# A gated linear recurrence: pairs of tokens within 32 in two rounds of column-tiled matmuls, sample states on four column tiles

## The chip, the cores and the metric

The kernel runs on one core of a Trainium2 chip. A core has TensorE (PE in the profile; PEld is its weight load), VectorE (DVE), ScalarE (ACT), GpSimd (POOL) and SyncE (SP), which issues DMAs. TensorE reads SBUF and writes PSUM. The metric is the device time of one launch in microseconds (us); lower is better. Everything is f32, or f32r, the one-pass form of f32 on TensorE, in which the large matmuls run three times over a high and a low part.

## The reference, cut to what matters

Two layers. Layer 0 mixes tokens by causal pooling, layer 1 by HGRN2, a gated linear recurrence; each is followed by a gated ConvFFN. 512 prompt tokens and 8 samples of 4 new tokens (with a state each) go through together. The change lies in the recurrence of layer 1, with 8 heads of 128 x 128:

```python
def step(S, xs):                       # per chunk, per head
    qc, kc, vc, gc = xs                # gc = log of the decay f
    b = jnp.cumsum(gc, axis=2)
    o_inter = jnp.einsum('bhtd,bhde->bhte', qc * jnp.exp(b), S)
    diff = b[:, :, :, None, :] - b[:, :, None, :, :]
    decay = jnp.where(causal, jnp.exp(jnp.where(causal, diff, 0.0)), 0.0)
    a = jnp.einsum('bhtd,bhsd,bhtsd->bhts', qc, kc, decay)
    o = o_inter + jnp.einsum('bhts,bhse->bhte', a, vc)
    ...
    S = jnp.exp(b_last[:, :, 0, :])[..., None] * S + jnp.einsum('bhsd,bhse->bhde', kc * jnp.exp(b_last - b), vc)
```

`a[t, s]` holds, for each pair of tokens with s <= t, the sum over 128 channels of q[t] k[s] times the product of the decays f between them.

## The kernel before, in words

**Order of work.** Every operation is recorded first (`Plan.record`, the only line of the profile with nearly all instructions, L304) with a cost in microseconds (`Plan.cost`), and a list scheduler (`Plan.emit`) then writes the engines' orders: of what is ready by its own estimate, the operation with the longest tail goes next. Between the matmuls of a projection (`block`, 48 matmuls of 256 or 288 columns), a `tick` after every three adds `PACE` to a counter, and each time it reaches 1 one more step of the recurrence is recorded. An engine keeps its written order: if an instruction's input is late, those behind it wait.

**Layer 1.** The projections for f, q, i and g of each head run as such blocks; after a head's i, `attention(h)` queues its steps: load, transposes, diag, seven levels, ktrans, states, output, sstates, back. Head after head, they are interleaved with the blocks of later heads.

**Pairs by levels.** The matrix `A` (per 128-token chunk, 128 x 128, s on partitions, t on columns) is put together by distance. `diag` gives pairs s = t: K^T q over a whole chunk, of which only the diagonal is kept, by a product with the identity. Level w (1, 2, 4, ..., 64) gives the pairs in which s lies in the left and t in the right half of a block of 2w tokens. For this q and K are scaled step by step, at level w each right half of q by the decays of the left block of w, and each left half of K by those of the right one (`qv`, `kv`); the block decays are products of two each (`fn`). A full chunk of K (128 weight columns) meets 64 columns of q, and DVE copies the wanted blocks of the 128 x 64 result into A under a mask (`copy_predicated`). diag and w = 1 share a matmul of 192 columns for each of four chunks (the columns of q and of the scaled q side by side in the tile `q2`); so do w = 4 and w = 8. From w = 16 (`BLKW`) each block is a matmul of its own, 128 x w by w, and ScalarE copies it into A. The 32 samples' tokens have their own diag, w = 1 and w = 2 matmuls (tile `As`).

**States and output.** `states` makes the chunk states S; `output` sums A V (4 matmuls), the samples' As V, the samples' q against their 8 states, each with a masked copy of q that is zero but for its 4 of 32 columns (`qm`, 8 matmuls on PSUM partitions 0 to 31), and q S (3). `back` transposes the normed result, 4 chunks and the samples' 32 rows.

**Names in rows.** `ps`: PSUM of the projections; `pa`: PSUM tiles of the recurrence and of grouped blocks; `pr`: PSUM of the norms (`colsums` adds up squares with 32 columns of ones, on PSUM partitions 0, 32, 64 and 96 in turn); `t`: a ring of 24 tiles (q, K, F, V, states, ...); `cs`: constants (identity, ones, masks); `wl`, `wh`: low and high part of weights; `fst`/`q2`: one tile that serves the FFN and the recurrence in turn; `lbm`: lower bounds; `R`: the norm's factors.

Of the kernel before, what the change touches and what calls it, by code (L numbers as in the profile page):

```python
# [17 lines left out]
P = 128  # L18
D = 1024
KT = 8  # L20
SEQ = 512
# [16 lines left out]
LEVELS = (1, 2, 4, 8, 16, 32, 64)  # L38
# [10 lines left out]
PACE = 0.3  # L49
MERGE = 4  # L50
BLKW = 16
# [16 lines left out]
C_ID, C_ONE, C_SB, C_MASK, C_BM = 0, 128, 256, 256 + 192, 256 + 192 + 448  # L68
NCST = C_BM + NB

class Plan:
# [84 lines left out]
    def cost(eng, name, args, kw):  # L156
# [181 lines left out]
def trunk_step(ctx: ExitStack, tc: _tile.TileContext, xT, xp, xs, spool, s0, fctx, par, gb0, cst, bands,  # L338
# [8 lines left out]
    tp = ctx.enter_context(tc.tile_pool(name="tp", bufs=24))  # L347
# [498 lines left out]
    def ffn(li, XH, XL, res, enter, mtile, leave, n_ahead, hv=HV):  # L846

        R = res.rnext
        cst_t = rp.tile([P, 2 * NPAIR * 18], F32, tag="fst", name="fst", bufs=1)
# [160 lines left out]

    def lower_bounds():
# [29 lines left out]
    qm = one.tile([P, NB * 36], F32, name="qm")  # L1041
    DVE.memset(qm, 0.0)
    q2 = rp.tile([P, 2 * NPAIR * 18], F32, tag="fst", name="q2", bufs=1)[:, 0:768]
# [32 lines left out]
    def attention(h):  # L1076
# [30 lines left out]
        def diag():  # L1107

            qq = q2.rearrange("p (c t) -> p c t", c=4)
            ACT.activation(qq[:, :, 0:P], q[:, 0:SEQ].rearrange("p (c t) -> p c t", c=4), AF.Identity)  # L1110
            pd = [ps1(), ps1()]
            PE.matmul(pd[1][0:NS, 384:384 + NS], samp(K), samp(q), start=True, stop=True, skip_group_check=True)
            DVE.tensor_tensor(q, q, F, op=ALU.mult)
            ACT.activation(qq[:, :, P:192], q[:, 0:SEQ].rearrange("p (c t r) -> p c t r", c=4, r=2)[:, :, :, 1], AF.Identity)
            A = tt((P, 4, P))
            As = sm.tile([P, NS], F32, tag="As", name="As", bufs=2)
            st["A"], st["As"] = A, As
            mk = cs[:, C_MASK:C_MASK + 64].bitcast(I32)
# [3 lines left out]
            PE.matmul(pd[1][0:NS, 384 + NS:384 + NS + HS], samp(K), samp(q).rearrange("p (n r) -> p n r", r=2)[:, :, 1],  # L1122
                      start=True, stop=True, skip_group_check=True)
            for a in range(2):
                v = pd[a][:, 0:384].rearrange("p (c t) -> p c t", c=2)
                Aa = A[:, 2 * a:2 * a + 2, :]
                DVE.tensor_tensor(Aa, v[:, :, 0:P], ident.unsqueeze(1).broadcast_to([P, 2, P]), op=ALU.mult)
                DVE.copy_predicated(Aa.rearrange("p c (t r) -> p c t r", r=2)[:, :, :, 1], mk.unsqueeze(1).broadcast_to([P, 2, 64]), v[:, :, P:192])
            DVE.tensor_tensor(As[0:NS], pd[1][0:NS, 384:384 + NS], ident[0:NS, 0:NS], op=ALU.mult)
            DVE.copy_predicated(As[0:NS].rearrange("p (n r) -> p n r", r=2)[:, :, 1], mk[0:NS, 0:HS],  # L1130
                                pd[1][0:NS, 384 + NS:384 + NS + HS])
            st["F"] = F
            st["fl"], st["fo"] = tt(), 0

# [3 lines left out]
        def level(li):  # L1138
            w = LEVELS[li]
            nb = 64 // w  # L1140
            if li and w not in (MERGE, MERGE * 2):
                pl = ps1()
            smp = w < 4
            if w in (1, MERGE * 2):
                pass
            elif w == MERGE:

                wide = st["wide"] = [ps1(), ps1()]
                z = q2.rearrange("p (c t) -> p c t", c=4)
                qc = q[:, 0:SEQ].rearrange("p (c t) -> p c t", c=4)  # L1150

                def half(t, v):
                    return t.rearrange("p c (n r v) -> p c n r v", r=2, v=v)[:, :, :, 1, :]
                ACT.activation(z[:, :, 0:64].rearrange("p c (n v) -> p c n v", v=w), half(qc, w), AF.Identity)
                F0 = st["F"][:, 0:SEQ // w].rearrange("p (c n) -> p c n", c=4)
                DVE.tensor_tensor(half(qc, w), half(qc, w), F0[:, :, 0::2].unsqueeze(3).broadcast_to([P, 4, nb, w]),
                                  op=ALU.mult)
                zb, zc = (z[:, :, a:a + 64].rearrange("p c (n v) -> p c n v", v=2 * w) for a in (64, 128))
                ACT.activation(zb, half(qc, 2 * w), AF.Identity)
                DVE.tensor_tensor(zc, half(qc, 2 * w), F0[:, :, 1::4].unsqueeze(3).broadcast_to([P, 4, nb // 2, 2 * w]),  # L1160
                                  op=ALU.mult)
                for c in range(4):
                    PE.matmul(wide[c // 2][:, (c % 2) * 192:(c % 2 + 1) * 192], chunk(K, c), z[:, c, :], start=True,
                              stop=True, skip_group_check=True)
                for a in range(2):
                    src = wide[a][:, 0:384].rearrange("p (c t) -> p c t", c=2)
                    Aa = st["A"][:, 2 * a:2 * a + 2, :]
                    for col, v, slot in ((0, w, li), (64, 2 * w, li + 1), (128, 2 * w, 5)):
                        mk = cs[:, C_MASK + slot * 64:C_MASK + (slot + 1) * 64].bitcast(I32)
                        DVE.copy_predicated(half(Aa, v), mk.rearrange("p (n v) -> p n v", v=v).unsqueeze(1).broadcast_to(  # L1170
                            [P, 2, 64 // v, v]), src[:, :, col:col + 64].rearrange("p c (n v) -> p c n v", v=v))
            elif w >= BLKW:

                for j in range(0, P, 2 * w):
                    for c in range(4):
                        PE.matmul(pl[j:j + w, c * w:(c + 1) * w], chunk(K, c)[:, j:j + w],
                                  chunk(q, c)[:, j + w:j + 2 * w], start=True, stop=True)
                for j in range(0, P, 2 * w):
                    ACT.activation(st["A"][j:j + w, :, j + w:j + 2 * w],
                                   pl[j:j + w, 0:4 * w].rearrange("p (c t) -> p c t", c=4), AF.Identity)  # L1180
            else:
                for c in range(4):
                    PE.matmul(pl[:, c * 64:(c + 1) * 64].rearrange("p (n w) -> p n w", w=w), chunk(K, c),
                              oddv(chunk(q, c), w)[:, :, 1, :], start=True, stop=True)
                mk = cs[:, C_MASK + li * 64:C_MASK + (li + 1) * 64].bitcast(I32)
                if smp:
                    PE.matmul(pl[0:NS, 256:256 + HS].rearrange("p (n w) -> p n w", w=w), samp(K),
                              oddv(samp(q), w)[:, :, 1, :], start=True, stop=True)
                mk4 = mk.rearrange("p (n w) -> p n w", w=w).unsqueeze(1).broadcast_to([P, 4, nb, w])
                Av = st["A"].rearrange("p c (n r w) -> p c n r w", r=2, w=w)[:, :, :, 1, :]  # L1190
                DVE.copy_predicated(Av, mk4, pl[:, 0:256].rearrange("p (c n w) -> p c n w", c=4, w=w))
                if smp:
                    DVE.copy_predicated(oddv(st["As"][0:NS], w)[:, :, 1, :],
                                        mk[0:NS, 0:HS].rearrange("p (n w) -> p n w", w=w),
                                        pl[0:NS, 256:256 + HS].rearrange("p (n w) -> p n w", w=w))

            Fw = st["F"]
            if w <= 2:
                nbt = TOK // (2 * w)
                qv, kv = oddv(q, w)[:, :, 1, :], oddv(K, w)[:, :, 0, :]  # L1200
                fv = Fw.rearrange("p (n r) -> p n r", r=2)
                fe = fv[:, :, 0:1].broadcast_to([P, nbt, w])
                fo = fv[:, :, 1:2].broadcast_to([P, nbt, w])
                Fn = st["fl"][:, st["fo"]:st["fo"] + nbt]
                st["fo"] += nbt
# [301 lines left out]
```

## Time and profile before

| | |
|---|---|
| Median of 3 runs (lowest to highest) | 1246.05 us (1242.43 to 1247.79) |
| Profiled execution: time, span | 1243.85 us, 1242.1 us |
| Granted TensorE clock | 0.994 |
| Time from HBM and to it | 110.95 MB read, 8.31 MB written, 96 GB/s over the span |
| Recurrence (windows of the trace) | about 503 to 769 us |

"Busy" is a share of the span; matmuls are pipelined, so what a matmul costs is told by the distance between starts, not by its length. A row of the timeline has the start, the time, the engine, the line, the operation, out<-in by the tiles' names, the form (rows * weight columns, then out) and the count; after [ ] stands idle time before it. An f32 matmul shows as two instructions there and as one in the written order.

### The profile page before, as it was taken

How to read it: one execution, taken by the hardware profiler on the slowest of the kernel's cores; microseconds unless marked ns; L12 is line 12 of the kernel's file. 1: busy time of each engine (PE TensorE's matmuls, PEld its weight loads, DVE VectorE, ACT ScalarE, POOL GpSimd, SP SyncE). 2: the span in 40 equal slices, each digit the busy share in tenths (PEclk: the TensorE clock that was granted, in tenths of full speed). 3: DMA queues.
4: the chain of work that ended last, by engine and by line, in shares of the span. 5: the costliest groups of instructions: out<-in, count | busy, mean ns of one | idle time of the engine just before them, and what ended most of it. 6: DMA issues, size and time to landing. Idle time of an engine off the chain costs nothing.

```text
span 1242.1 us, 24777 instructions
## 1 busy us (share of the span) xinstructions
PE 1223.4 (98%) x9932; PEld 1187.3 (96%) x9932; DVE 795.1 (64%) x1834; ACT 545.3 (44%) x1083; POOL 212.2 (17%) x510
## 2 busy tenths in 40 slices
PE   8999999999999999999999999999999999999996
PEld 7899999999999988999999999999999999999995
DVE  6787725774577565677777887376762566457745
ACT  4754434442344554444444444465443344234441
POOL 3331101110011141011111211143110111011113
PEclk9999999999999999999999999999999999999998
DMA  9622222222222463322222123364222222322202
GB/s 324 155 88 85 86 85 86 96 78 90 96 84 92 153 142 71 102 80 79 80 96 80 63 71 100 102 137 101 87 85 97 88 85 75 100 86 89 84 29 72
DMA packets 43218, 120.49 MB, mean 97 GB/s; under 512 B 5338, under 2 KB 9818, under 8 KB 43096
## 3 DMA queue, kind: packets, MB, share of 16 engines
q1 hardware_dynamic: 30336, 91.87, 22.5%
q0 software_dynamic: 12624, 27.01, 9.1%
q8 instruction: 78, 1.28, 0.4%
q14 instruction: 36, 0.29, 0.1%
q10 hardware_dynamic: 144, 0.05, 0.0%
HBM read 110.95 MB, written 8.31 MB: 96 GB/s over the span
## 4 chain that ended last, share of the span: by engine, by line
PE 95%; DVE 2%; DMA 2%; ACT 1%; issue 0%; SPq 0%; DVEq 0%; ACTq 0%
PE ps L304 73%; PE pa L304 20%; PE pr L304 2%; DVE m L304 1%; DVE t L304 1%; DMA k<-xp 1%; DMA t<-pw 1%; DMA k<-wup 0%; ACT t L304 0%; SPq L304 0%; ACT wh L304 0%; DVE c L304 0%; ACT m L304 0%; DVE x L304 0%; DVEq L1488 0%
## 5 line engine op out<-in xcount | busy, mean ns | idle before, releaser
L304 ACT ACTIVATE wh<-raw 128x512 fp32r<-128x512 f32 (+1 forms) x312 | 193.1, 620 | 342.4 <-PE ps L304 330.9
L304 PE MATMUL ps<-xh,wh 128*128 128x256 f32 (+1 forms) x1072 | 312.4, 292 | 0.0
L304 PE MATMUL ps<-xh,wl 128*128 128x256 f32 (+1 forms) x1072 | 311.7, 291 | 0.0
L304 PE MATMUL ps<-xl,wh 128*128 128x256 f32 (+1 forms) x1072 | 311.5, 291 | 0.0
L304 DVE TENSOR_TENSOR wl<-raw,wh 128x512 fp32r<-128x512 f32 (+1 forms) x312 | 210.3, 675 | 133.1 <-ACT wh L304 129.2
L304 PE MATMUL ps<-t,wh 128*128 128x272 f32 x1184 | 223.4, 288 | 0.9 <-ACT m L304 0.7
L304 PEld LDWEIGHTS ps<-xh,wl 128*128 128x128 f32 x1072 | 202.2, 189 | 2.4 <-issue 1.4
L304 PEld LDWEIGHTS ps<-xh,wh 128*128 128x128 f32 x1072 | 201.6, 188 | 2.5 <-issue 1.3
L304 PEld LDWEIGHTS ps<-xl,wh 128*128 128x128 f32 x1072 | 202.2, 189 | 1.2 <-issue 0.5
L304 PE MATMUL ps<-oh,wl 128*128 128x256 f32 (+2 forms) x688 | 198.1, 288 | 0.0
L304 PE MATMUL ps<-k,wh 128*128 128x256 f32 (+2 forms) x688 | 197.7, 287 | 0.0
L304 PE MATMUL ps<-oh,wh 128*128 128x256 f32 (+2 forms) x688 | 197.3, 287 | 0.0
L304 DVE TENSOR_TENSOR t<-t 128x512 f32<-128x512 f32 (+7 forms) x332 | 146.4, 461 | 63.8 <-ACT t L304 45.0
L304 PEld LDWEIGHTS ps<-t,wh 128*128 128x128 f32 x1184 | 185.4, 188 | 1.8 <-ACT m L304 1.2
L304 DVE SCALAR_TENSOR_TENSOR t<-t,prm 128x560 f32<-128x560 f32 (+1 forms) x184 | 147.6, 805 | 35.7 <-ACT t L304 32.9
L304 PE MATMUL ps<-t,wl 128*128 128x272 f32 x592 | 170.3, 288 | 0.0
L304 POOL COPY fst<-t 128x2 f32<-128x2 f32 (+1 forms) x176 | 72.9, 443 | 442.9 <-DVE t L304 442.6
L304 DVE TENSOR_TENSOR t<-ps,R 128x512 f32<-128x512 f32 (+1 forms) x216 | 86.2, 434 | 77.1 <-PE ps L304 73.2
L304 PEld LDWEIGHTS ps<-k,wh 128*128 128x128 f32 x688 | 129.5, 188 | 0.5 <-issue 0.5
L304 PEld LDWEIGHTS ps<-oh,wl 128*128 128x128 f32 x688 | 129.7, 188 | 0.0
L304 PEld LDWEIGHTS ps<-oh,wh 128*128 128x128 f32 x688 | 129.6, 188 | 0.0
L304 ACT ACTIVATE t<-t 128x560 f32<-128x560 f32 (+4 forms) x137 | 83.1, 616 | 95.5 <-DVE t L304 94.5
(169 smaller groups left out, 1703.9 us busy)
## 6 DMA issues: line engine op xcount, KB each, us to landing
raw<-wup SPq DMA_DIRECT2D x78, 512.0 KB, 3.3
raw<-wdn SPq DMA_DIRECT2D x32, 448.0 KB, 3.3
raw<-win SPq DMA_DIRECT2D x26, 512.0 KB, 3.3
raw<-wdn SPq DMA_DIRECT2D x16, 512.0 KB, 3.2
wh<-wup POOLq DMA_DIRECT2D x16, 256.0 KB, 4.0
wl<-wup POOLq DMA_DIRECT2D x16, 256.0 KB, 5.1
t<-s POOLq DMA_DIRECT2D x16, 256.0 KB, 3.9
o_hs<-t POOLq DMA_DIRECT2D x16, 256.0 KB, 2.4
```

Source lines behind the costliest of these rows:

```text
L304: o[1](*o[3], **o[4])
```

## The change

Pairs within 32 tokens no longer use whole chunks. diag and the levels 1 to 8 become two rounds over the 16 blocks of 32 tokens: a matmul has one block's 32 columns of K as weights, and block g of a chunk writes PSUM partitions 32g to 32g + 31, so that four consecutive matmuls use the four column tiles of the array. Round A (diag, w = 1, w = 2; 80 columns) also takes the 32 samples' tokens as a 17th block; round B (w = 4, w = 8) has 48 columns. The pairs between the first and last quarter of a block of four (or 16) come from columns scaled once more (`zv(64, 2)`, `zv(32, 8)`). Results are collected in a tile `Al` of 4 x 32 columns under masks of 32 columns, then four ScalarE copies put them into the blocks on the diagonal of A. A is now one tile for all heads, zeroed once on GpSimd, as is qm, which holds two groups of four samples. The samples' q times state go four at a time to four column tiles, each with 32 columns (4 samples' tokens in the second half, others in the first); As is split likewise; the way back transposes 128 rows. Recording is paced at 0.25 instead of 0.3 with 12 steps in place of 15, the ring t has 22 tiles, and the planner's cost of narrow matmuls is another.

```diff
-LEVELS = (1, 2, 4, 8, 16, 32, 64)
+LOCAL = 32
+ROUND_A, ROUND_B = 80, 48
-PACE = 0.3
+PACE = 0.25
...
-                return n / 2400 + 0.01
+                return max(n / 2400 + 0.01, 0.0018 * m)
...
-    tp = ctx.enter_context(tc.tile_pool(name="tp", bufs=24))
+    tp = ctx.enter_context(tc.tile_pool(name="tp", bufs=22))
...
+                POOL.memset(A, 0.0)
+                POOL.memset(qm, 0.0)
...
-        def diag():
...
-            for c in range(4):
-                PE.matmul(pd[c // 2][:, (c % 2) * 192:(c % 2 + 1) * 192], chunk(K, c), qq[:, c, :], start=True,
-                          stop=True, skip_group_check=True)
...
+        def round_a():
+            z = q2[:, 0:17 * ROUND_A].rearrange("p (b t) -> p b t", t=ROUND_A)
...
+            ACT.activation(z[:, :, 0:LOCAL], q.rearrange("p (b t) -> p b t", t=LOCAL), AF.Identity)
+            DVE.tensor_tensor(q, q, F, op=ALU.mult)
+            ACT.activation(zv(32, 1), by_block(upper(q, 1)), AF.Identity)
+            scale(q, 1, 1, F)
+            hi = by_block(upper(q, 2))
+            ACT.activation(zv(48, 2), hi, AF.Identity)
+            DVE.tensor_tensor(zv(64, 2), hi, by_block(quarter(F, 1, 1)).broadcast_to([P, 17, 8, 2]), op=ALU.mult)
+            pl = ps1()
+            for c in range(4):
+                for g in range(4):
+                    b = 4 * c + g
+                    PE.matmul(pl[32 * g:32 * g + 32, c * ROUND_A:(c + 1) * ROUND_A], K[:, 32 * b:32 * b + 32], z[:, b, :],
+                              start=True, stop=True, skip_group_check=True)
+            PE.matmul(pl[0:NS, 4 * ROUND_A:5 * ROUND_A], samp(K), z[:, 16, :], start=True, stop=True, skip_group_check=True)
+            Al = sm.tile([P, 4, LOCAL], F32, tag="Al", name="Al", bufs=2)
...
+            scale(K, 1, 0, F)
+            products(1)
+            scale(q, 2, 1, st["F"])
+            scale(K, 2, 0, st["F"])
+            products(2)
...
+        def round_b():
...
+            for c in range(4):
+                for g in range(4):
+                    b = 4 * c + g
+                    PE.matmul(pl[32 * g:32 * g + 32, c * ROUND_B:(c + 1) * ROUND_B], K[:, 32 * b:32 * b + 32], z[:, b, :],
+                              start=True, stop=True, skip_group_check=True)
...
+            for j in range(0, P, LOCAL):
+                ACT.activation(A[j:j + LOCAL, :, j:j + LOCAL], st["Al"][j:j + LOCAL], AF.Identity)
...
         def output():
...
-            PE.matmul(po2[0:NS, 0:P], st["As"][0:NS], st["Vs"][0:NS], start=True, stop=False)
-            for b in range(NB):
-                PE.matmul(po2[0:NS, 0:P], st["qm"][:, b * NS:(b + 1) * NS], st["s0"][b // 4][:, b % 4, :],
-                          start=False, stop=(b == NB - 1))
...
+            for a in range(2):
+                for g in range(4):
+                    PE.matmul(po2[32 * g:32 * g + 32, 0:P], qm[:, a, g, :], st["s0"][a][:, g, :], start=(a == 0), stop=False,
+                              skip_group_check=True)
+            for g in range(4):
+                PE.matmul(po2[32 * g:32 * g + 8, 0:P], st["As"][0:NS, 8 * g:8 * g + 8], st["Vs"][0:NS], start=False, stop=True,
+                          skip_group_check=True)
...
-            PE.transpose(pq2[:, 0:NS], st["ons"][0:NS], ident[0:NS, 0:NS])
+            PE.transpose(pq2[:, 0:P], st["ons"], ident)
```

What TensorE's written order holds for the first head's pairs up to the level w = 16, before (`q_861` is the tile q2; the lines left out are projection matmuls):

```order
L304 MATMUL pa<-t 32x32
...
L304 MATMUL pa<-t 32x16
...
L304 MATMUL pa<-q_861,t 128x192 x4
...
L304 MATMUL pa<-t 128x64 x4
L304 MATMUL pa<-t 32x16
...
L304 MATMUL pa<-q_861,t 128x192 x4
...
L304 MATMUL pa<-t 16x16 x16
```

And the same piece of the changed order (`q_862` is q2); between the two rounds stand 16 projection matmuls:

```order
L304 MATMUL pa<-q_862,t 32x80 x17
...
L304 MATMUL pa<-q_862,t 32x48 x16
...
L304 MATMUL pa<-t 16x16 x16
```

Five bursts ahead of w = 16 have become two, and the samples' bursts of one matmul are gone.

The first head's output on TensorE, before:

```order
L304 MATMUL pa<-t 128x128 x8
L304 MATMUL pa<-t,As 32x128
L304 MATMUL pa<-t,qm 32x128 x8
L304 MATMUL pa<-t 128x128 x3
```

and after, where the state products (`states`) stand 12 projection matmuls ahead:

```order
L304 MATMUL pa<-t 128x128 x4
...
L304 MATMUL pa<-t,A 128x128 x4
L304 MATMUL pa<-t 128x128 x3
L304 MATMUL pa<-t,qm 32x128 x8
L304 MATMUL pa<-t,As 8x128 x4
```

The samples' products moved behind the full-width ones, and As is four narrow matmuls.

VectorE's changed order around the first head's rounds; the first four rows stand between round A and round B (K scaled, q scaled, K scaled, q2 written), the others after them:

```order
L304 TENSOR_TENSOR t<-t 128x272
L304 TENSOR_TENSOR t<-t 128x64x4
L304 TENSOR_TENSOR t<-t 128x136x2
L304 TENSOR_TENSOR q_862<-t 128x16x16
L304 TENSOR_TENSOR Al<-pa,cs 128x128
L304 TENSOR_TENSOR t<-t 128x32x8
L304 TENSOR_TENSOR As<-pa,cs 32x2x4x4
L304 COPY_PREDICATED Al<-cs,pa 128x64
L304 COPY_PREDICATED As<-cs,pa 32x2x4x2
L304 TENSOR_TENSOR t<-ps,R_226 128x512
```

What round B needs was put ahead of the masked copies of round A's results.

More of the change, by code (lines that the diff above doesn't have):

```diff
@@ L848, in ffn @@
         R = res.rnext
-        cst_t = rp.tile([P, 2 * NPAIR * 18], F32, tag="fst", name="fst", bufs=1)
+        cst_t = rp.tile([P, 17 * ROUND_A], F32, tag="fst", name="fst", bufs=1)[:, 0:2 * NPAIR * 18]
         if li == 0:
@@ L1009, in trunk_step @@
     lbm = one.tile([P, 8, KT], F32, name="lbm")
+    A = one.tile([P, 4, P], F32, name="A")
+    qm = one.tile([P, 2, 4, LOCAL], F32, name="qm")
     def lower_bounds():
@@ L1040, in trunk_step @@
     hd = {}
-    qm = one.tile([P, NB * 36], F32, name="qm")
-    DVE.memset(qm, 0.0)
-    q2 = rp.tile([P, 2 * NPAIR * 18], F32, tag="fst", name="q2", bufs=1)[:, 0:768]
+    q2 = rp.tile([P, 17 * ROUND_A], F32, tag="fst", name="q2", bufs=1)
     def proj(ps):
@@ L1105, in transposes @@
             st["V"], st["Vst"], st["Vs"] = V, VV[:, 0, :], VV[:, 1, :]
-        def diag():
[L1109 to L1118, printed above, removed]
-            for c in range(4):
-                PE.matmul(pd[c // 2][:, (c % 2) * 192:(c % 2 + 1) * 192], chunk(K, c), qq[:, c, :], start=True,
-                          stop=True, skip_group_check=True)
[L1122 to L1133, printed above, removed]
@@ L1135, in oddv @@
         def oddv(t, w):
             return t.rearrange("p (n r w) -> p n r w", r=2, w=w)
[L1138 to L1172, printed above, removed]
-                for j in range(0, P, 2 * w):
[L1175 to L1205, printed above, removed]
-                f0, f1, fn = fv[:, :, 0], fv[:, :, 1], Fn
-            else:
-                nbt = SEQ // (2 * w)
-                qv, kv = oddv(q[:, 0:SEQ], w)[:, :, 1, :], oddv(K[:, 0:SEQ], w)[:, :, 0, :]
-                fv = Fw[:, 0:2 * nbt].rearrange("p (n r) -> p n r", r=2)
-                fe = fv[:, :, 0:1].broadcast_to([P, nbt, w])
-                fo = fv[:, :, 1:2].broadcast_to([P, nbt, w])
-                Fn = st["fl"][:, st["fo"]:st["fo"] + nbt]
-                st["fo"] += nbt
-                f0, f1, fn = fv[:, :, 0], fv[:, :, 1], Fn
-            if w != MERGE:
-                DVE.tensor_tensor(qv, qv, fe, op=ALU.mult)
-            DVE.tensor_tensor(kv, kv, fo, op=ALU.mult)
-            DVE.tensor_tensor(fn, f0, f1, op=ALU.mult)
-            st["F"] = Fn
-            if w == 2:
-                st["F4"] = Fn
@@ new lines, in quarter, with upper, products, scale @@
+        def quarter(t, w, r):
+            return t.rearrange("p (n r w) -> p n r w", r=4, w=w)[:, :, r, :]
+        def upper(t, w):
+            return oddv(t, w)[:, :, 1, :]
+        def products(w):
+            f = st["F"].rearrange("p (n r) -> p n r", r=2)
+            n = f.shape[1]
+            fn = st["fl"][:, st["fo"]:st["fo"] + n]
+            st["fo"] += n
+            DVE.tensor_tensor(fn, f[:, :, 0], f[:, :, 1], op=ALU.mult)
+            st["F"] = fn
+        def scale(t, w, r, f):
+            tv = oddv(t, w)[:, :, r, :]
+            fv = f.rearrange("p (n r) -> p n r", r=2)[:, :, 1 - r:2 - r].broadcast_to(list(tv.shape))
+            DVE.tensor_tensor(tv, tv, fv, op=ALU.mult)
@@ new lines, in level @@
+        def level(w):
+            pl = ps1()
+            for c in range(4):
+                for j in range(0, P, 2 * w):
+                    PE.matmul(pl[j:j + w, c * w:(c + 1) * w], chunk(K, c)[:, j:j + w], chunk(q, c)[:, j + w:j + 2 * w],
+                              start=True, stop=True, skip_group_check=True)
+            for j in range(0, P, 2 * w):
+                ACT.activation(A[j:j + w, :, j + w:j + 2 * w], pl[j:j + w, 0:4 * w].rearrange("p (c t) -> p c t", c=4), AF.Identity)
+            scale(q[:, 0:SEQ], w, 1, st["F"])
+            scale(K[:, 0:SEQ], w, 0, st["F"])
+            products(w)
@@ L1264, in output @@
                           skip_group_check=True)
+            for a in range(2):
+                for g in range(4):
[4 more added lines that the diff above has]
+                          skip_group_check=True)
             on, ons = tt((P, 4, P)), tt((P, P))
             ss, r, w, z, a, b = (sm.tile([P, 5], F32, tag=f"o{q}", name="o", bufs=2) for q in range(6))
-            DVE.memset(ss[:, 4:5], 0.0)
             for c in range(4):
                 ACT.activation(on[:, c, :], po[:, c * P:(c + 1) * P], AF.Square, accum_out=ss[:, c:c + 1])
-            ACT.activation(ons[0:NS], po2[0:NS, 0:P], AF.Square, accum_out=ss[0:NS, 4:5])
+            ACT.activation(ons, po2[:, 0:P], AF.Square, accum_out=ss[:, 4:5])
             rstd_into(r, ss, 1.0 / P, w, z, a, b)
@@ L1295, in back @@
                 PE.transpose(pq[:, c * P:(c + 1) * P], st["on"][:, c, :], ident)
-            PE.transpose(pq2[:, 0:NS], st["ons"][0:NS], ident[0:NS, 0:NS])
+            PE.transpose(pq2[:, 0:P], st["ons"], ident)
             o = kslot(F32)
             ACT.activation(o[:, 0:SEQ], pq, AF.Identity)
-            ACT.activation(o[:, SEQ:TOK], pq2[:, 0:NS], AF.Identity)
+            ACT.activation(o[:, SEQ:TOK].rearrange("p (h g t) -> p g h t", h=2, g=4),
+                           pq2[:, 0:P].rearrange("p (g x) -> p g x", g=4)[:, :, 0:8].rearrange("p g (h t) -> p g h t", h=2), AF.Identity)
             hd[h]["on"] = o
-        return [load, transposes, diag] + [lambda li=li: level(li) for li in range(len(LEVELS))] + \
+        return [load, transposes, round_a, round_b] + [lambda w=w: level(w) for w in (16, 32, 64)] + \
             [ktrans, states, output, sstates, back]
```

79 lines of the change are left out of this document (64 added, 15 removed).

## The prediction

> **What bounds the kernel now.** I read the page first (busy shares, then the chain of waits), then the windows of the stage that the change touches, then TensorE's waits in it, and last its timeline.
>
> ```profile
> PE 1223.4 (98%) x9932; PEld 1187.3 (96%) x9932; DVE 795.1 (64%) x1834; ACT 545.3 (44%) x1083; POOL 212.2 (17%) x510
> PE 95%; DVE 2%; DMA 2%; ACT 1%; issue 0%; SPq 0%; DVEq 0%; ACTq 0%
> 503.00:769.00 266.00, 265.00 (x2360) 249.98 (x2359) 202.85 (x603) 115.67 (x344) 37.26 (x67) 1.00 0.24 81
> PE pa L304 <- DVE t L304: 1.0, 2, 0.7
> ```
>
> The second row is the chain of waits by engine: 95% of the span is TensorE following TensorE. The third is the stretch in which the eight heads' recurrences run (columns: length, then busy time and count of PE, PEld, DVE, ACT and POOL, granted clock, DMA share, GB/s): PE is busy 265.0 of 266.0 us at full clock. The fourth is all that PE waits there, 1.0 us in two waits. So a microsecond of TensorE work taken out of this stage is a microsecond off the end, as long as VectorE and ScalarE still deliver in time; and the whole question is what the matmuls of the recurrence cost TensorE before and after.
>
> **What they cost before.** The recurrence's matmuls stand as small bursts between the 256- and 288-column matmuls of the projection. This is the timeline of PE for the first head (start, time, form, instructions; an f32 matmul shows as two, called passes here).
>
> ```profile
> 504.85 0.28 PE L304 MATMUL ps<-xl,wh 128*128 128x256 f32 x1
> 504.97 0.28 PE L304 MATMUL ps<-xh,wl 128*128 128x256 f32 x1
> 505.18 0.25 PE L304 MATMUL pa<-t 128*32 128x32 f32 x2
> 505.35 0.40 PE L304 MATMUL ps<-xh,wh 128*128 128x288 f32 x1
> 505.59 0.29 PE L304 MATMUL ps<-xl,wh 128*128 128x288 f32 x1
> 505.72 0.29 PE L304 MATMUL ps<-xh,wl 128*128 128x288 f32 x1
> ...
> 507.30 0.23 PE L304 MATMUL pa<-t 128*32 128x16 f32 x2
> ...
> 508.06 1.46 PE L304 MATMUL pa<-q,t 128*128 128x192 f32 x8
> 509.22 0.43 PE L304 MATMUL ps<-xh,wh 128*128 128x288 f32 x1
> 509.49 0.29 PE L304 MATMUL ps<-xl,wh 128*128 128x288 f32 x1
> ...
> 510.61 1.17 PE L304 MATMUL pa<-t 128*128 128x64 f32 x10
> 511.71 0.39 PE L304 MATMUL ps<-xl,wh 128*128 128x256 f32 x1
> 511.93 0.28 PE L304 MATMUL ps<-xh,wl 128*128 128x256 f32 x1
> ...
> 515.20 1.46 PE L304 MATMUL pa<-q,t 128*128 128x192 f32 x8
> ```
>
> A projection matmul's own pace is 0.12 us at 256 columns (504.85 to 504.97) and 0.13 at 288 (505.59 to 505.72). A burst's price is what it adds to that pace. The samples' 32x32 matmul: from 504.97 to 505.59 pass 0.62 us, of which 0.12 + 0.13 are two projection matmuls, so it costs 0.37, although its arithmetic is tiny. The 16-column one (507.30) is the same burst with 0.23 us in place of 0.25: 0.35. The burst of four 192-column products: 509.49 - 508.06 - 0.13 = 1.30; the second one, same form and same 1.46, again 1.30. The w=2 level: 511.93 - 510.61 - 0.12 = 1.20. All five go: 0.37 + 0.35 + 1.30 + 1.30 + 1.20 = 4.52 us per head.
>
> **What the two rounds cost.** They are 17 matmuls of 32 weight columns by 80, and 16 of 32 by 48, laid on four column tiles in turn. No row shows this; the nearest are the column sums of the norms, which use 32 ones-columns on the four tiles, and the w=16 level.
>
> ```profile
> 450.42 0.62 PE L304 MATMUL pr<-t,cs 128*32 128x256 f32 x2
> 450.96 0.40 PE L304 MATMUL pa<-t,wh 128*128 128x288 f32 x1
> ...
> 816.91 0.64 PE L304 MATMUL pr<-t,cs 128*32 128x256 f32 x8
> 817.48 0.40 PE L304 MATMUL pa<-oh,wl 128*128 128x288 f32 x1
> ...
> 518.09 0.73 PE L304 MATMUL pa<-t 128*16 128x16 f32 x32
> 518.75 0.40 PE L304 MATMUL ps<-xl,wh 128*128 128x288 f32 x1
> ```
>
> One 256-column sum holds PE for 0.54 us until the next full-width matmul (450.42 to 450.96), four on four tiles for 0.57 (816.91 to 817.48). So the tiles stream side by side, and three more matmuls cost 0.03. A pass takes 1.30 / 8 / 192 = 0.85 ns per column (from the 192-column burst), so a 256-column sum streams 2 x 0.217 = 0.435, and the rest of the burst's price is the turn into and out of the tiled form: the 0.37 of the 32x32 matmul less its 2 x 0.027 is 0.31.
>
> Round A: tile 0 holds five matmuls (four blocks and the samples), 10 passes x 80 x 0.85 ns = 0.68, + 0.31 + 0.02 for the other tiles' start = 1.01 us. Round B: 8 passes x 48 x 0.85 ns = 0.33, + 0.31 + 0.03 = 0.67. The upper end is no overlap at all: 34 x 0.068 + 0.31 = 2.62 and 32 x 0.041 + 0.31 = 1.62. I take the lower values, since the four-tile row is the nearest in form; both ends stay for the rivals.
>
> A rule speaks against the small passes. The Trainium skill, "TensorE: Matmul & The Clock Gate", section "Wait — 56ns, not 53.3ns?", has matmuls never start less than about 25 ns apart. Were that a floor over all tiles, the rounds would be 34 x 0.025 and 32 x 0.025 + 0.31 each, estimated from that page 1.16 and 1.11 instead of 1.01 and 0.67, and the total 4.7 us later. The w=16 level does not bear it out: 32 passes fit in 0.66 us (518.09 to 518.75), 20.6 ns each, with its turn included.
>
> **The other parts.**
>
> ```profile
> 524.53 0.71 PE L304 MATMUL pa<-cs,t 128*128 128x128 f32 x5
> 525.00 0.36 PE L304 MATMUL ps<-xl,wh 128*128 128x256 f32 x1
> 525.20 0.28 PE L304 MATMUL ps<-xh,wl 128*128 128x256 f32 x1
> ...
> 527.95 0.40 PE L304 MATMUL pa<-t,As 32*32 32x128 f32 x2
> 528.28 1.93 PE L304 MATMUL pa<-t,qm 128*32 128x128 f32 x16
> 530.15 0.94 PE L304 MATMUL pa<-t 128*128 128x128 f32 x6
> ...
> 766.96 0.78 PE L304 MATMUL pa<-cs,t 128*128 128x128 f32 x5
> 767.67 0.39 PE L304 MATMUL ps<-xl,wh 128*128 128x256 f32 x1
> ```
>
> Samples' states: today 16 passes on one tile, 528.28 to 530.15, at 128 x 0.85 ns = 0.109 each 1.74 us. On four tiles it is four passes deep, 0.44: a gain of 1.30. The four `As` matmuls of 8 columns replace one of 32 (527.95 to 528.28, turn included); side by side they cost 0.02 more, one behind the other 3 x 0.22 = 0.65. I take 0. The output burst turns form three times before and after. Way back: the samples' 32-row transpose makes a burst of 0.71 us (766.96 to 767.67), one with a full-width fifth transpose 0.47 (524.53 to 525.00): a gain of 0.24. A burst that stands alone adds 525.20 - 525.00 - 0.12 = 0.08 at its border; in the new order the state products stand apart from the output in every head and the first transposes apart from the way back, about 12 borders more: +1.0 us in all. One more column sum of the norm before the first heads stands alone: 450.42 to 450.96 and its turn, 0.31 + 0.44 = +0.75. The two waits, 1.0 us, belong to the 16-column matmul that goes: -1.0.
>
> VectorE, ScalarE, GpSimd:
>
> ```profile
> 536.00:568.60 32.60, 32.60 (x293) 30.75 (x292) 24.19 (x79) 13.65 (x42) 3.81 (x6) 1.00 0.23 81
> 701.30:767.00 65.70, 65.02 (x583) 61.37 (x582) 55.66 (x147) 30.99 (x88) 11.61 (x31) 1.00 0.26 82
> ...
> L304 DVE TENSOR_TENSOR t<-t 128x256 f32<-128x256 f32 x10 | 3.9, 419 | 1.7 <-PE pa L304 1.6
> L304 DVE COPY_PREDICATED t<-cs,pa 128x128 f32<-128x128 int32 x8 | 2.3, 331 | 0.0
> L304 DVE TENSOR_TENSOR t<-pa,cs 128x256 f32<-128x256 f32 x2 | 0.8, 421 | 0.2 <-PE pa L304 0.2
> L304 DVE COPY_PREDICATED t<-cs,pa 128x256 f32<-128x256 int32 x1 | 0.7, 736 | 0.0
> L304 DVE COPY_PREDICATED As<-cs,pa 32x16 f32<-32x16 int32 x2 | 0.5, 232 | 0.0
> ...
> 11.74 0.58 POOL L304 DMA_DIRECT2D k<-wup  x1 [3.76 <-issue]
> ```
>
> The first row is one head's 32.6 us (DVE busy 24.19, ACT 13.65), the second the last two heads (55.66 of 65.7); the group rows are the DVE's in the first. The masked results go from 2.3 + 0.8 + 0.7 + 0.5 = 4.3 us to six copies of 64 columns (between the 32x16's 0.23 and the 128x128's 0.29, say 0.26: 1.6), one product of 128 columns (0.35), four small ones for the samples (0.9) and one more scaled copy for q2 (0.39): 3.2. DVE gains 1.1 us a head, the head's time falls to 28.2, so its share rises from 74 to 82%, and with the last two heads from 85 to (27.8 - 1.1) / 28.5 = 94%. That is the cover which thins. In the new order 16 projection matmuls, 2.0 us, stand between the rounds; behind round A, DVE scales K twice and q once and writes q2 before round B can start, four of 0.39 = 1.6 us, and a ScalarE copy of q in parallel. That fits, with 0.4 to spare; behind the late heads' 94% it may not always. Allowance: between 0 and, one such 0.39 late in half the 40 tiled bursts, 8 us; as TensorE waited 1.0 us in all at 85%, I take +1.5. ScalarE's added q2 and A copies (some 1.5 us a head) leave it near half busy. The A and qm memsets stand on GpSimd ahead of the first weight DMA at 11.74, in an idle stretch of 3.76 us; what fits there costs nothing, and were they longer, that DMA and the ones queued behind it would start late. Two fewer t buffers and the smaller mask load move nothing in the order outside the recurrence: 0.
>
> **The sum.** Per head -4.52 + 1.01 + 0.67 - 1.30 - 0.24 = -4.38; eight heads -35.0. With +1.0 + 0.75 - 1.0 + 1.5 = +2.3 that is -32.7 from the profiled execution's 1243.85 us: 1211. That execution lies 2.2 us under the median of the three runs (1246.05), inside their spread; the same shift on the after side would give 1213, which the range covers. Less than 0.5% (6 us) can't be told from no change here.
>
> **The rivals.**
> 1. *Passes in program order.* The same page of the Trainium skill, section "Part 3: Packing small matmuls — row/col tiling", calls matmuls strictly first in, first out. As a mechanism here: an f32 matmul's second pass must wait for its first on the same tile, so if the next tile's first pass could not overtake it, only neighbours would overlap, and n matmuls would take n + 1 pass times. Round A 18 x 0.068 + 0.31 = 1.53, round B 17 x 0.041 + 0.31 = 1.01, the states 9 x 0.109 = 0.98 (a gain of 0.76), As 5 x 0.109 in place of 0.22 (+0.33): -4.52 + 1.53 + 1.01 - 0.76 + 0.33 - 0.24 = -2.65 a head, -21.2, and with the +2.3 from above 1225. Against it: four column sums would then take 5 x 0.217 = 1.09, and the row shows 0.57. By that rule 1225; the trace disagrees with it where there are four matmuls, and no row shows it for 17.
> 2. *VectorE sets the pace.* Against: 1.0 us of waits now. For: 94% in the last heads. With its 0.39 in half the bursts: 1211 - 1.5 + 8 = 1217.
> 3. *No overlap.* Round A 2.62, B 1.62, states 0, As +0.65: -4.52 + 2.62 + 1.62 + 0.65 - 0.24 = +0.13, and 1243.85 + 1.0 + 2.3 = 1247: no change. Against: the same four-tile row.
> 4. *A change of column tile is a turn of its own* (the other side). If every step to the next tile drained the array like half of the 0.31 in and out, 45 steps a head x 0.155 = 7.0 us, and no overlap: 1247 + 56 = 1303. It makes the kernel over 0.5% slower from about 3 / (8 x 45), 8 ns a step. Against: three such steps cost 0.03 us in the sums, side by side at that.
>
> **How the numbers follow.** The forecast (1206 to 1215) 0.60; rival 1 or something between, to 1225, 0.17; rival 2, 0.15; rival 3, 0.05; rival 4, 0.03. So faster by over 0.5% 0.92, the same 0.05, slower 0.03. Low end 1204: no waits, no new borders (1208.6), and the runs' spread of 2 to 4 us below; high end 1225, rival 1. Rivals 3 and 4 stay out, and with what lies beyond those ends some 0.15 is left out.
>
> **What would show it.** Right: the 80-column burst holds TensorE about 0.9 us to the next full-width matmul and the 48-column one 0.55 (their prices less the 0.1 that lies ahead of a burst); qm's 16 passes near 0.6 instead of 1.87; bursts of five transposes at 0.47; a head every 28 us. Rival 1: 1.4 and 0.9. Rival 2: PE's waits on DVE or ACT of several us between 480 and 740 us. The prediction is wrong if passes of 17 matmuls don't overtake as four do, or if VectorE falls behind.

## The result and the profile after

The changed kernel takes 1205.8 us (median of 4 runs, 1205.18 to 1207.21) beside 1244.24 us for the kernel before (4 runs on the same chip, 1242.34 to 1247.79): a ratio of 0.9689, 95% interval 0.9662 to 0.9717, or 38.4 us less. The profiled execution is the slowest of the four, 1207.21 us, 36.6 less than the profiled one of before. One execution of all those used below, in experiment 5, took 2396.56 us where the other four of its kernel took 1210.01 to 1212.55; it is left out.

First the page of the changed kernel (busy shares, the chain of waits by engine), then the windows of the stretch with the heads and TensorE's waits in it, which answer to the first four rows of the prediction.

```profile
PE 1184.2 (98%) x10268; PEld 1148.4 (95%) x10268; DVE 784.5 (65%) x1809; ACT 558.9 (46%) x1131; POOL 214.1 (18%) x512
PE 95%; DVE 2%; DMA 1%; ACT 0%; issue 0%; SPq 0%; DVEq 0%; POOL 0%; ACTq 0%; POOLq 0%
503.00:734.00 231.00, 229.40 (x2719) 214.51 (x2718) 193.90 (x588) 129.84 (x391) 39.73 (x72) 1.00 0.28 93
PE pa L304 <- DVE q L304: 0.9, 1, 0.9
PE pa L304 <- ACT t L304: 0.3, 1, 0.3
```

TensorE is still the bound (95% of the chain). The stretch with the heads has 231 us where it had 266 (with 1236 projection matmuls in it against 1214, so the two are not quite the same work), DVE is busy 84% of it (76% before), and the shown waits are still about 1 us. A head comes every 27.5 us instead of 32.9 (the 80-column bursts of the first two heads start at 505.48 and 532.94). Of that difference 0.7 us is no gain: 144 projection matmuls stand between two heads where 150 did, since 12 steps at a pace of 0.25 take 48 ticks and 15 steps at 0.3 took 50.

The bursts of the first head in the timeline of PE after:

```profile
505.26 0.29 PE L304 MATMUL ps<-xh,wl 128*128 128x288 f32 x1
505.48 0.88 PE L304 MATMUL pa<-q,t 128*32 128x80 f32 x34
506.29 0.39 PE L304 MATMUL ps<-xh,wh 128*128 128x256 f32 x1
...
508.47 0.55 PE L304 MATMUL pa<-q,t 128*32 128x48 f32 x32
508.95 0.41 PE L304 MATMUL ps<-xl,wh 128*128 128x288 f32 x1
...
510.65 0.38 PE L304 MATMUL pa<-t 128*16 128x16 f32 x32
510.96 0.40 PE L304 MATMUL ps<-xl,wh 128*128 128x288 f32 x1
...
512.67 0.45 PE L304 MATMUL pa<-t 128*32 128x32 f32 x16
513.04 0.40 PE L304 MATMUL ps<-xl,wh 128*128 128x288 f32 x1
...
520.89 1.05 PE L304 MATMUL pa<-t,A 128*128 128x128 f32 x8
521.78 0.83 PE L304 MATMUL pa<-t 128*128 128x128 f32 x6
522.54 0.65 PE L304 MATMUL pa<-t,qm 128*32 128x128 f32 x16
523.11 0.40 PE L304 MATMUL pa<-t,As 32*8 32x128 f32 x8
523.44 0.38 PE L304 MATMUL ps<-xh,wh 128*128 128x256 f32 x1
```

Round A holds TensorE 506.29 - 505.48 = 0.81 us to the next full-width matmul, round B 0.48, qm's 16 passes 0.57 (522.54 to 523.11) where they took 1.87. As prices over the projections' pace that is 1.01 for round A (forecast 1.01) and 0.68 for B (forecast 0.67). What the forecast did not have is the next pair of bursts: w = 16 holds 0.31 us here and 0.66 before, w = 32 holds 0.37 here and 0.52 before. Their matmuls are the same ones as before.

### The profile page after: what moved, and what is told of

It reads as the page before. It is cut to its first block, busy times and chain, and to the rows that moved or that the text cites. A ratio compares the mean times of both kernels' runs of the same rounds, so it can differ in the third digit from the quotient of the medians.

```text
span 1205.4 us, 25491 instructions
## 1 busy us (share of the span) xinstructions
PE 1184.2 (98%) x10268; PEld 1148.4 (95%) x10268; DVE 784.5 (65%) x1809; ACT 558.9 (46%) x1131; POOL 214.1 (18%) x512
## 4 chain that ended last, share of the span: by engine, by line
PE 95%; DVE 2%; DMA 1%; ACT 0%; issue 0%; SPq 0%; DVEq 0%; POOL 0%; ACTq 0%; POOLq 0%
PE ps L304 75%; PE pa L304 18%; PE pr L304 2%; DVE t L304 1%; DVE m L304 1%; DMA t<-bands 1%; DMA k<-wup 0%; SPq L304 0%; DVE c L304 0%; ACT wh L304 0%; ACT m L304 0%; DVE x L304 0%; DVE Al L304 0%; DVEq L1513 0%; ACT t L304 0%
## 5 line engine op out<-in xcount | busy, mean ns | idle before, releaser
L304 PE MATMUL ps<-xh,wl 128*128 128x256 f32 (+1 forms) x1072 | 307.2, 287 | 0.0
L304 DVE TENSOR_TENSOR t<-t 128x512 f32<-128x512 f32 (+10 forms) x332 | 141.2, 453 | 55.5 <-ACT t L304 45.9
L304 POOL COPY fst<-t 128x16 f32<-128x16 f32 (+1 forms) x176 | 73.0, 450 | 440.6 <-DVE t L304 440.3
```

The lines of the kernel that those rows point to most:

```text
L304: o[1](*o[3], **o[4])
```

## The experiments

Below, a burst's price is again what it adds to the projections' pace; sums are over the eight heads of one profiled execution. Times are medians; each set of runs has its own runs of the kernel before (1243.7 to 1245.3 us), so ratios compare best between sets.

**1. Why w = 16 and w = 32 fell.** In `level` of the changed kernel the loop over the four chunks stands outside and that over the blocks inside; before it was the other way round. Since a block's place sets its column tile, consecutive matmuls now change tiles. First the order is put back in the kernel after, then the swap alone is made in the kernel before:

```diff
-            for c in range(4):
-                for j in range(0, P, 2 * w):
+            for j in range(0, P, 2 * w):
+                for c in range(4):
```

> The changed kernel, but the levels w = 16, 32 and 64 loop over the blocks j outside and over the chunks c inside, as before: four matmuls in a row on one column tile. Theory (the deepest tile sets a burst's time, and a pass overtakes waiting ones only within a short reach): the w = 16 burst goes from 0.52 us back to 0.85, w = 32 from 0.57 to 0.72, w = 64 stays at 0.80; 0.47 us a head, 3.8 us in all, to about 1209.6 us, ratio to before near 0.972. Rival (these bursts became shorter for another cause, such as what stands around them): bursts stay at 0.52 and 0.57, ratio 0.969.

Measured 1209.63 us (1208.49 to 1211.34), ratio 0.9726 (0.9711 to 0.9740). The timeline of PE there:

```profile
507.89 0.72 PE L304 MATMUL pa<-t 128*16 128x16 f32 x32
508.54 0.40 PE L304 MATMUL ps<-xl,wh 128*128 128x288 f32 x1
...
510.25 0.59 PE L304 MATMUL pa<-t 128*32 128x32 f32 x16
510.77 0.40 PE L304 MATMUL ps<-xl,wh 128*128 128x288 f32 x1
```

The bursts hold 0.65 and 0.52 us again; the other bursts keep their prices.

> The kernel before, with only the two loops of the matmuls of the levels 16 and 32 swapped (chunks outside, blocks inside), so that one after the other go to different column tiles; nothing else moves. Theory (tiles overlap only when the order of issue alternates them): the w=16 burst goes from 0.85 to 0.52 us and the w=32 burst from 0.715 to 0.57, 0.475 a head, 3.8 in all: 1240.4 beside 1244.2, ratio 0.997. Rival (the gain of the loops needs the rest of the change, such as another place in the order): 1244.2, ratio 1.000, bursts as before.

Measured 1240.0 us (1238.32 to 1242.0), ratio 0.9966 (0.9952 to 0.9979). The first head's two bursts:

```profile
516.46 0.39 PE L304 MATMUL pa<-t 128*16 128x16 f32 x32
516.78 0.40 PE L304 MATMUL ps<-xl,wh 128*128 128x288 f32 x1
...
518.24 0.45 PE L304 MATMUL pa<-t 128*32 128x32 f32 x16
518.62 0.39 PE L304 MATMUL ps<-xh,wl 128*128 128x256 f32 x1
```

So the order of two loops is worth about 4 us in either kernel, by itself: the same work on the same tiles, issued so that the tiles take turns.

**2. What the rounds' gain hangs on.** The same question put to the rounds: tile after tile instead of in turn, and all blocks on one tile.

```diff
-            for c in range(4):
-                for g in range(4):
+            for g in range(4):
+                for c in range(4):
```

> The changed kernel, but rounds A and B go tile by tile: the four blocks of tile 0, then those of tile 1, and so on; the matmuls are the same. Short reach (a new tile starts when about three passes of the tile ahead still wait, as in the w = 16 burst of before): round A 3 x 5 x 0.069 + 8 x 0.069 + 0.31 = 1.90 us in place of 1.01, round B 1.25 in place of 0.68, 1.46 a head, 11.7 us in all, to 1217.5. Overtaking without limit: no change, 1205.8. Strict program order (overlap only where two neighbours lie on two tiles): 2.45 and 1.50, 18 us, to 1224.

```diff
-                    PE.matmul(pl[32 * g:32 * g + 32, c * ROUND_A:(c + 1) * ROUND_A], ...
+                    PE.matmul(pl[0:32, c * ROUND_A:(c + 1) * ROUND_A], ...
```

> The changed kernel, but all blocks of rounds A and B write PSUM partitions 0 to 31, so that all matmuls share column tile 0 (the blocks overwrite each other's results, and the copies out of PSUM and into A work on those 32 partitions: A is not what it should be). Theory: no overlap is left, round A 34 x 0.069 + 0.31 = 2.66 us, round B 32 x 0.041 + 0.31 = 1.62, 2.6 a head, 20.7 us in all, to 1226.5. Rival (the rounds are bound by weight loads or by issue, whatever the tile): bursts stay near 1.0 and 0.7, 1206.

Tile after tile: 1215.14 us (1213.49 to 1217.53), ratio 0.9770 (0.9754 to 0.9787). One tile: 1225.31 (1224.9 to 1226.66), ratio 0.9854 (0.9837 to 0.9870). The two rounds of the first head, tile after tile first, then on one tile:

```profile
506.32 1.66 PE L304 MATMUL pa<-q,t 128*32 128x80 f32 x34
507.91 0.38 PE L304 MATMUL ps<-xh,wh 128*128 128x256 f32 x1
...
510.09 1.13 PE L304 MATMUL pa<-q,t 128*32 128x48 f32 x32
511.15 0.40 PE L304 MATMUL ps<-xl,wh 128*128 128x288 f32 x1
```

```profile
503.88 2.54 PE L304 MATMUL pa<-q,t 128*32 128x80 f32 x34
506.35 0.39 PE L304 MATMUL ps<-xh,wh 128*128 128x256 f32 x1
...
508.53 1.55 PE L304 MATMUL pa<-q,t 128*32 128x48 f32 x32
510.01 0.40 PE L304 MATMUL ps<-xl,wh 128*128 128x288 f32 x1
```

On one tile the prices are 2.67 and 1.68: each pass for itself, 69 ns from start to start in round A, 19.5 us more in all. So neither weight loads nor issue, which are as many on one tile, set the rounds' price. Tile after tile the prices are 1.78 and 1.26, between the two. The starts of the single records tell how. In turn, four passes start 7 ns apart, and one group of four follows the other by 69 ns (the second follows the first by 94), which is one pass of 80 columns. Tile after tile, four passes start alone (506.319, 506.412, 506.481, 506.551); right behind the fifth (506.620) another one starts (506.626), and from there on two start in each 69 ns. The records don't name the tile, but with all passes on one tile no two start within a pass time, so I read it as the next tile's first pass. It overtakes three passes of the tile ahead that still wait, and that is how far the overtaking reaches here: the first starts of the tiles lie 0.31 us apart. What sets this reach isn't shown. The Trainium skill, "TensorE: Matmul & The Clock Gate", section "Part 3: Packing small matmuls — row/col tiling", calls matmuls strict first in, first out; read as "nothing behind a waiting pass starts", the records disagree with it, and 1.78 us would have been 2.45. The 25 ns between starts that the prediction weighed show up on each tile (in the w = 16 burst of the kernel after, groups of four follow each other by 25 ns), but not over tiles (7 ns within a group; 32 passes of w = 16 in 0.31 us).

**3. Does an emptier tile matter?** Round A's samples make tile 0 five matmuls deep, the others four. Three more matmuls fill the others:

```diff
+            for g in range(1, 4):
+                PE.matmul(pl[32 * g:32 * g + 32, 4 * ROUND_A:5 * ROUND_A], K[:, 32 * g:32 * g + 32], z[:, g, :], start=True,
+                          stop=True, skip_group_check=True)
```

> The changed kernel with three more matmuls at the end of round A, of blocks 1 to 3 once more, to tiles 1 to 3 beside the samples' matmul on tile 0 (results unused). Deepest tile: the burst of 80 columns grows by three starts of 7 ns, from 0.81 to 0.83 us to the next full-width matmul. Sum of passes: by 6/34 of 0.70, to 0.93. In order: three passes more, 0.207, to 1.02. Time within noise of 1206.

Measured 1206.24 us in one run; round A with 40 passes:

```profile
503.73 0.90 PE L304 MATMUL pa<-q,t 128*32 128x80 f32 x40
504.56 0.38 PE L304 MATMUL ps<-xh,wh 128*128 128x256 f32 x1
```

It holds TensorE 0.83 us and has a price of 1.02, where 34 passes have 0.81 and 1.01. The deepest tile sets the burst's time, as the prediction's sum had it.

**4. The samples' part alone,** put into the kernel before:

```diff
-            for b in range(NB):
-                PE.matmul(po2[0:NS, 0:P], st["qm"][:, b * NS:(b + 1) * NS], st["s0"][b // 4][:, b % 4, :], ...
+            for a in range(2):
+                for g in range(4):
+                    PE.matmul(po2[32 * g:32 * g + 32, 0:P], qm[:, a, g, :], st["s0"][a][:, g, :], ...
```

> The kernel before, with only the samples' part of the output put on four column tiles (states, the four As matmuls, a fifth transpose at full width), and one small VectorE copy a head that regroups As. Theory (the states are four passes deep, and the part has its price by itself): 10.3 us of the output bursts and 1 to 2 us of the transposes, 11 to 12 in all: 1232 to 1233, ratio 0.991. Rival 1 (passes overlap only with their neighbour, so the states gain 0.76 and As costs 0.33 more): -0.76 + 0.33 - 0.24 = -0.67 a head, -5.4: 1239, ratio 0.9957. Rival 2 (the gain hangs on the pair rounds, which leave VectorE the time): waits of several us on VectorE, above 1239.

Measured 1237.45 us (1237.09 to 1238.97), ratio 0.9944 (0.9931 to 0.9958): 7.3 us where the theory had 11 to 12, and neither rival's bursts. The first head's output:

```profile
528.26 0.41 PE L304 MATMUL pa<-t,qm 128*32 128x128 f32 x2
528.59 0.49 PE L304 MATMUL pa<-t 128*128 128x128 f32 x2
529.01 0.64 PE L304 MATMUL pa<-t,qm 128*32 128x128 f32 x14
529.58 0.40 PE L304 MATMUL pa<-t,A 32*8 32x128 f32 x8
```

The four tiles work, but the planner set one qm matmul ahead of the last product of q and S, which by its estimate waits for DVE. TensorE turns into the tiled form, out and in again: 0.75 us for 2 + 2 passes (528.26 to 529.01) that take about 0.3 inside bursts (after: 0.57 for 16 of qm, 0.76 for 6 of q and S). Seven such splits stand in the eight heads. Next, qm is held behind that product:

```diff
+            last = len(plan.ops) - 1
             for a in range(2):
                 for g in range(4):
+                    plan.held = {last}
```

> The kernel with only the samples' states changed (e6), and its eight states matmuls made to wait for the head's last product of q and S, so that the planner can't set one or two of them ahead of it. Theory (every further turn into and out of the tiled form costs about what it costs ahead of a burst; the 2 passes of qm and 2 of q and S that stand apart take 0.75 us where they would take 0.25): 7 splits x 0.5 = 3.5 us, 1234, ratio to before 0.991. Rival (the split filled a wait for S that is there anyway): 1237 to 1238, with the wait or the border showing ahead of the last product.

Measured 1236.91 us (1236.28 to 1239.03), ratio 0.9940 (0.9927 to 0.9953): the rival's side, and no clear change from the 1237.45 without the hold. The two rows on DVE's and ScalarE's results in TensorE's waits, without the hold and with it:

```profile
PE pa L304 <- DVE t L304: 2.3, 4, 1.0
PE pa L304 <- ACT wh L304: 0.3, 2, 0.2
```

```profile
PE pa L304 <- DVE t L304: 4.1, 7, 1.0
PE pa L304 <- ACT wh L304: 1.7, 2, 0.9
```

State products and output fell by 3.5 us, from 32.1 to 28.6, which is the theory's 7 x 0.5. But the transposes rose by 2.6, from 15.9 to 18.5: six of the way back's bursts now wait 0.6 to 0.9 us, put down to DVE four times and to ScalarE twice. What the split cost was real, and most of it covered a wait. Output and state products at 28.6 are 10.2 us below the 38.8 of the kernel before, as the theory for this part had it; the time gains less because the transposes wait (18.5 us against 14.9) and so does the level w = 2 (two waits of 0.5 and 1.0 us on DVE), so the part doesn't have its price by itself.

**5. What the planning numbers are worth.** `PACE` and the planned cost of a narrow matmul only move instructions. Both at their old values in the kernel after; then with qm held together as above; then the old cost alone.

```diff
-PACE = 0.25
+PACE = 0.3
...
-                return max(n / 2400 + 0.01, 0.0018 * m)
+                return n / 2400 + 0.01
```

> The kernel after with the old planning numbers: PACE 0.3 and the old planned cost of a matmul with 32 weight columns (the t buffers stay at 22). Theory (the numbers only place the bursts; the gain is in the bursts themselves): every burst at the price it has in the kernel after, 1203 to 1209, the difference being waits and lone borders. Rival (the numbers are a part of the gain, since they keep VectorE ahead of TensorE): TensorE's waits in the heads grow from about 3 to 6 us or more, 1209 to 1214.

> The kernel after with the old planning numbers (e8), and its eight states matmuls made to wait for the head's last product of q and S. Theory (of the 8.8 us that the old numbers cost, the split output bursts are the larger part: 9 splits x 0.5 = 4.5): 1210, the rest being waits for S and for the rounds' inputs. Rival (the split only filled waits): 1214 to 1215.

> The kernel after with the old planned cost of a matmul with 32 weight columns and the new PACE of 0.25. The planner now sets a head's last product of q and S between the first and the second of the four As matmuls, in every head; the places of the heads stay apart by the same pace. Theory (a burst split once costs about 0.5 us whatever the pace, and the waits at the way back and the rounds go with PACE): 8 x 0.5 = 4.0 us above the kernel after, 1209 to 1210, output bursts near 3.05 us to the next projection matmul and no more waits than after. Rival 1 (PACE carries it all): 1206. Rival 2 (the planned cost carries it all): 1213 to 1215.

Measured: both old, 1214.56 us (1213.53 to 1216.09), ratio 0.9760 (0.9747 to 0.9774); held together, 1211.66 (1210.01 to 1212.55), ratio 0.9734 (0.9720 to 0.9748), between theory and rival; the old cost alone, 1211.62 (1210.87 to 1214.3), ratio 0.9727 (0.9711 to 0.9744). The output of the first head with the old cost alone:

```profile
522.89 0.64 PE L304 MATMUL pa<-t,qm 128*32 128x128 f32 x16
523.46 0.38 PE L304 MATMUL pa<-t,As 32*8 32x128 f32 x2
523.77 0.49 PE L304 MATMUL pa<-t 128*128 128x128 f32 x2
524.19 0.39 PE L304 MATMUL pa<-t,As 32*8 32x128 f32 x6
524.51 0.39 PE L304 MATMUL ps<-xh,wh 128*128 128x256 f32 x1
```

Both old numbers cost 8.8 us: the rival is right, and short by a little. Round A keeps its price of 1.01 us; round B waits 0.7 to 1.2 us in each of the last three heads, where after waits in two. State products and output rise from 28.5 to 35.5 us; nine splits make the larger part of that. Held together, the two fall by 4.7, and the time by 2.9: the rest returns as waits, as in experiment 4. With the old cost alone six of eight heads are split, not all eight: five as shown, one inside qm. Their output bursts cost 3.0 us more, 0.5 a split, as expected. The time is 1 to 2 us above the theory's 1209 to 1210, which had no further waits: in this trace the state products cost 2.8 us more than after, as in seven of the eight heads they start 0.2 to 0.5 us behind the projections' pace; the longest of these waits is listed, behind a result of ScalarE. In all the old cost is worth 4.7 us by the ratios (0.9727 less 0.9689). The remaining 4.1 us (0.9760 less 0.9727) I put down to PACE; no run changes PACE alone.

**6. A further version.** The levels 32 and 64 write odd chunks to the other column tiles, and a norm's four column sums wait for all four squares instead of the one recorded last, which ScalarE did not always make last:

```diff
+            side = 0 if w == 16 else w
...
+                    r = j + side * (c % 2)
+                    PE.matmul(pl[r:r + w, c * w:(c + 1) * w], chunk(K, c)[:, j:j + w], chunk(q, c)[:, j + w:j + 2 * w],
...
-            plan.after(sqs[ks[-1]])
+            held = set()
+            for q in ks:
+                plan.after(sqs[q])
+                held |= plan.held
+            plan.held = held
```

> A further version. (a) The levels 32 and 64 write the odd chunks to the other column tiles (four of 32 columns, two of 64), with 3 more ScalarE copies a head; (b) the four column sums of a norm wait for all their four squares, so that they are issued together. Theory (the deepest tile sets a burst's time, and the turn of 0.31 us is paid once a burst): w=64 from 0.80 to 0.31 + 4 x 0.054 + 0.02 = 0.55, w=32 from 0.57 to 0.31 + 4 x 0.027 + 0.03 = 0.45, 0.37 a head, -3.0; eight lone sums of 0.77 us each join a burst for 0.03, -6.0: 1197, ratio to the kernel before 0.962. Rival (the later first sums and the added copies are waited for): the bursts as said, but waits take half or more of it back, 1201 or above.

Measured 1201.53 us (1199.36 to 1203.73), ratio 0.9655 (0.9639 to 0.9671), the rival's side of 1201. The bursts came as said: w = 64 from 0.80 to 0.58, w = 32 from 0.57 to 0.46, the sums some 7 us less. TensorE waits 1.1 us for GpSimd once, at an update of the samples' states in the first head; the rest of what was lost shows at the state products, here in the first head of this version and of the kernel after:

```profile
510.11 0.29 PE L304 MATMUL ps<-xh,wl 128*128 128x288 f32 x1
510.50 1.16 PE L304 MATMUL pa<-t 128*128 128x128 f32 x8
```

```profile
518.36 0.29 PE L304 MATMUL ps<-xh,wl 128*128 128x288 f32 x1
518.50 1.05 PE L304 MATMUL pa<-t 128*128 128x128 f32 x8
```

The burst starts 0.39 us behind the projection matmul instead of 0.14. The profile lists no idle time for it: it models a matmul's end (510.11 + 0.29 = 510.40), which leaves 0.10 us. The distance between starts shows it, in every head, 3.4 us in all. In two later heads the wait is long enough to be listed, behind ScalarE's copies. So one change is taken back, `side = w if w == 64 else 0`, which leaves one added copy a head:

> The further version (e9) without its change of the level 32: level 64 on two column tiles with one more ScalarE copy a head, and the column sums in fours. Theory (in e9 the state products waited 0.2 to 0.35 us a head and once 0.78 for ScalarE's copy of the transposed K, behind the three added copies; with one added copy most of that goes, 3.4 less 0.9 for the level): about 1199, ratio to before 0.963. Rival (the wait comes with the later place of the state products or with any added copy): 1201.5 to 1202.5.

Measured 1198.4 us (1197.55 to 1199.94), ratio 0.9630 (0.9616 to 0.9644): the state products cost 7.9 us instead of 10.6, and this version is the fastest of all, 46 us under the kernel before and 7.4 under the kernel after.

## Why the prediction was right, point by point

It forecast 1211 us, 32.7 below its profiled execution; that of the kernel after lies 36.6 below. The median of 1205.8 lies just under the 1206 to 1215 that the forecast held likeliest, and inside its ends of 1204 and 1225. The mechanism came as forecast; the gain was under-forecast because two parts of it had no term: the loops of the levels 16 and 32, and some 2 us of the projections' own pace (last section). Over the eight heads, from the bursts of the two traces:

| step | forecast | measured |
|---|---|---|
| pairs below 16, with the two waits that go | -23.7 | -22.7, in which +1.3 is late round B |
| output, states and As | -10.4, and part of the +1.0 for borders | -10.3 |
| transposes | -1.9, and the rest of the borders | -0.4, in which about +1.3 is waits |
| levels 16 and 32 | nothing | -3.5 |
| one more lone column sum | +0.75 | +0.6 |
| VectorE late | +1.5 | about +3 of waits, already in the rows above (0.35 in w = 16) |

The measured rows add up to -36.3; with the 2 us of the projections' pace that is about the 38.4 of the medians.

- **Rounds A and B** came within 0.02 us of their forecast prices. Rival 1 (passes in program order, 1225) had 1.53 and 1.01 for the rounds, and experiment 2 speaks against its mechanism: even tile after tile the passes overtake. Rival 3 (no overlap) and rival 4 (a drain at every change of tile) fall with the 7 ns between starts; without overlap the rounds cost what they do on one tile, 2.67 and 1.68.
- **The samples' states** came as forecast. What the prediction did not say is that this holds only while they stay in one burst behind the products of q and S; experiments 4 and 5 put 0.5 us on each split. It read the written order of after and was right for it without naming the condition.
- **The step that failed** is that its list of the pairs that change price ends below w = 16, with the levels from 16 up left at nothing. The swap of loops in `level` stood in the changed kernel (not among the diff's lines shown), the prediction gave no term for it, and it is the largest miss: 3.5 us in the trace, 3.8 and 4.75 by the medians of experiment 1. The trace of before held the clue: the w = 16 burst's price of 0.85 us, less the turn of 0.31, leaves 17 ns for each of 32 passes, more than 16 columns take by themselves (13.6 at 0.85 ns a column), although the level uses four tiles.
- **VectorE late** was mis-sized: about 3 us of waits, not 1.5, and not all of it on VectorE. Round B waits in the last two heads (0.9 us on DVE and 0.3 on ScalarE in the listed rows), where the prediction had DVE 94% busy. The way back's first five heads wait about 0.2 us each, which no row lists, so what for is not shown:

```profile
526.89 0.29 PE L304 MATMUL ps<-xh,wl 128*128 128x288 f32 x1
527.23 0.74 PE L304 MATMUL pa<-cs,t 128*128 128x128 f32 x5
527.73 0.37 PE L304 MATMUL ps<-xh,wh 128*128 128x256 f32 x1
...
720.25 0.29 PE L304 MATMUL ps<-xh,wl 128*128 128x288 f32 x1
720.38 0.71 PE L304 MATMUL pa<-cs,t 128*128 128x128 f32 x5
720.84 0.36 PE L304 MATMUL ps<-xh,wh 128*128 128x256 f32 x1
```

  The first starts 0.34 us behind a projection matmul whose pace is 0.13, the last head's at that pace. Rival 2 is thus in the result with its small end, as far as these waits are VectorE's.
- **Outside the heads** the profiled execution of after waits 4.0 us for DVE at the very start, that of before 1.9. The kernels of experiments 1 to 6 show 2.1 to 3.9 there; I take it for the spread of one execution. Without it the two profiled executions differ by 38.7, which fits the medians' 38.4.

## What to carry to other kernels

Small matmuls on column tiles run fully side by side only if the written order changes tile from one to the next: swapping two loops was worth 4 us here, and 9 us for the rounds. Keep such a burst in one piece, since every interruption by full-width work cost TensorE about half a microsecond here, and check it in the written order whenever a planner's numbers change. Read waits from the distances between TensorE's starts, not only from listed idle time.

## What the runs showed of the hardware that I had not expected

- A waiting pass is overtaken by passes of another tile, as far as three waiting passes (experiment 2: two starts in each 69 ns from the fifth pass on).
- A 288-column projection matmul away from bursts took 132.0 ns on average in all ten traces of kernels with the rounds, and 132.7 to 132.8 in all four without them; the 256-column one 117.8 and 117.6. Over 3144 matmuls of each form that is some 2 us of the gain. The granted clock is the same (0.994 in both profiled executions). The cause stays open; the layout of SBUF, which the kernels of each family share, is a guess that no run tests.
